# Two token tiles ahead of the adaLN weights, and adaLN weights stored tile by tile

## The chip, the core and the metric

The kernel runs on one core of a Trainium2 chip. Its time is that of one execution on the device in microseconds (us). The median of three runs is 1481.48 us, the lowest 1479.01, the highest 1484.4. The engines are TensorE (PE; its weight loads are listed as PEld), VectorE (DVE), ScalarE (ACT), GpSimd (POOL) and SyncE (SP), which here only issues transfers.

## The reference, cut to what matters

A block of a diffusion transformer over 1024 latent tokens (`x`) and 256 context tokens (`ctx`), 1024 wide, depth 1. All is float32.

```python
sh1, sc1, g1, sh2, sc2, g2 = adaln(c, ada_w, ada_b)          # silu(c) @ ada_w + ada_b, split in six
csh1, csc1, ... = adaln(c_ctx[None, :], ada_w, ada_b)
h_lat = modulate(rms_norm(x, norm_mix_g), sh1, sc1)          # h * (1 + scale) + shift
h_ctx = modulate(rms_norm(x_ctx, norm_mix_g), csh1, csc1)
y = hybrid_mixer(h_ctx, h_lat, w_in, ...)                    # [context ; latent] @ w_in, DeltaNet and retention
x = x + g1 * (y[:, CTX_LEN:] @ w_out)
x = x + g2 * swiglu(modulate(rms_norm(x, norm_ffn_g), sh2, sc2), w_ffn_in, w_ffn_out)
return rms_norm(x, final_g)
```

The change concerns the first lines: the 1024 x 6144 matrix `ada_w` times two conditioning vectors, and the normalised, scaled and shifted tokens that the first projection reads.

## The kernel before, in words

Large products are made from three products of rounded parts: a float32 tile is split into `hi` (rounded to the matmul type by ACT, L344) and `lo` (the difference, by DVE, L345), and PE adds hi\*hi, lo\*hi and hi\*lo (L371 to L373, the tile `tm`). The tokens are handled in ten tiles of 128, of which 0 and 1 are context and 2 to 9 latent, in the groups [2, 3], [4, 5], [6, 7, 8, 9], [0, 1] (`XGROUPS`).

**The order of work.** The program text is laid out by a planner (the TileContext is opened with `schedule_with_timeline_sim=True`): it fixes the order on every engine beforehand by a simulated time, in which text order counts and readiness too, so an engine's queue may differ from the text. Each engine runs its queue in order. Two things are tied by hand. `in_order` (L235) chains the transfers on SP that go through it, so that they are issued in the order of the text; SP transfers that don't go through it (`weights`, L354) are placed among them by the planner. `tc.issue_after` sets one instruction behind another on its engine.

**The first stage.** It needs sixteen adaLN tiles of 128 x 2 x 512 floats (512 KB each). `ada_load(h, k)` (L254) takes, of the rows k\*128 to k\*128+127 of `ada_w`, columns from the shift and from the scale (i) for one half h of the 1024 features. In the matrix a row of the tile is two pieces of 512 floats, 2 KB each. The tiles share six buffers (`adaw`, bufs=6), so from the seventh on a load waits until an earlier tile is used up. `ada_tile(h, k)` (L258) multiplies a tile with the conditioning vectors: for six of the sixteen (`PLAIN`: (0,0), (0,7), (1,0), (1,1), (1,4), (1,7)) by direct float32 products on PE (L266, L268), for the others by an ACT rounding (`adahi`, L273), a DVE difference (`adalo`, L274) and products with both (L277, L278). The last tile of a half completes two PSUM rows; `rows_of` copies them out, `rows_turned` transposes them on PE, and `coefficients` (L293) makes scale and shift of that half on DVE.

`load_x(t)` (L240) loads one token tile of 128 rows of 4 KB, into one of seven buffers. `normalize(0)` squares tiles 2 and 3 on ACT (L325), makes the root (L126, with the loading of an ACT table) and its reciprocal on DVE, and scales the tiles (L328). They are transposed on PE (L334) and copied to `xnT` by DVE and ACT in turn (L422, L424). `modulate` (L307) applies the coefficients for one k and writes `hhi` (ACT, L311) and `hlo` (DVE L313, then DVE or POOL L314).

In the text before, all of half 0 comes first, then the first tile of half 1, then normalising and transposing, the split of the first raw weights, and the modulation of k = 0 to 3, mixed with the rest of half 1. The loads run in the order (0,0) to (0,7), (1,0), x2, x3, (1,1), (1,2), first raw weights, (1,3), (1,4), second raw weights, (1,5) to (1,7). The first product with the projection weights, `begin(2)` (L434, L443), is set behind the last product of tile (1,7); it is the first `tm` product of the kernel. Meanwhile the loads of the second weight group, the tiles 4 and 5 and further tokens follow on SP (L450 to L458). A prefetch of later weights (`wraw<-wg`, L354) shares two `wraw` buffers with the first two raw weights.

**Later adaLN tiles.** `ada_rest` (L488) is called eight times for the other four of the six parts. Each call loads four tiles of 128 x 2 x 512 by SP (L495) and sums them on DVE (L497, L499), beside the projections. There each row of a tile is two pieces of 2 KB too.

Of the kernel before, what the change touches and what calls it, by code (L numbers as in the profile page):

```python
# [17 lines left out]
P = 128  # L18
D = 1024
KT = D // P  # L20
# [18 lines left out]
def build(nc, tc, ap, dbg=None, stop=None, marks=None):  # L39
    root = ExitStack()  # L40
    V, S, G, T, SY = nc.vector, nc.scalar, nc.gpsimd, nc.tensor, nc.sync
# [45 lines left out]
    def bank(tag, name):  # L87
        return PS["pool"].tile([P, 512], F32, tag=tag, name=name, bufs=PS["tags"][tag])
# [4 lines left out]
    def bank_b(name):  # L93
        return bank("pb", name)
# [96 lines left out]
    try:  # L191
# [43 lines left out]
        def in_order(out, src):  # L235

            with tc.issue_after(order[0]) if order[0] is not None else nullcontext():
                order[0] = SY.dma_start(out, src).ins

        def load_x(t):  # L240
            xts[t] = P0.tile([P, D], F32, tag="xt", name="xt", bufs=7)
            in_order(xts[t], ap["ctx"][t * P:(t + 1) * P, :] if t < 2 else ap["x"][(t - 2) * P:(t - 1) * P, :])
# [10 lines left out]

        def ada_load(h, k):  # L254
            w = adaw[h, k] = PA.tile([P, 2, 512], F32, tag="adaw", name="adaw", bufs=6)
            in_order(w, ap["ada_w"][k * P:(k + 1) * P, 0:2 * D].rearrange("p (i e n) -> p i e n", i=2, e=2)[:, :, h, :])

        def ada_tile(h, k):  # L258
            w = adaw[h, k]
            kw = {"skip_group_check": True} if k else {}  # L260
            last = KT - 1
            if (h, k) in PLAIN:

                for i in range(2):
                    if k == 0:
                        T.matmul(psr[h][i][:4, :], cs0, w[:, i], start=True, stop=True)  # L266
                    else:
                        mm = T.matmul(psr[h][i][:2, :], csl[:, k, :], w[:, i], start=False, stop=(k == last), **kw)  # L268
                        done[0] = mm.ins
                return  # L270
            whi = PA.tile([P, 2, 512], F32R, tag="adahi", name="adahi", bufs=3)
            wlo = PA.tile([P, 2, 512], F32R, tag="adalo", name="adalo", bufs=3)
            S.activation(whi, w, AF.Copy)  # L273
            V.tensor_tensor(wlo, w, whi.bitcast(F32), ALU.subtract)  # L274
            for i in range(2):
                o = psr[h][i][:4, :]
                T.matmul(o, cs2[:, k].rearrange("p a b -> p (a b)"), whi[:, i], start=(k == 0), stop=False, **kw)  # L277
                T.matmul(o, cs2[:, k].rearrange("p a b -> p (a b)"), wlo[:, i], start=False, stop=True, **kw)  # L278

        def rows_of(h):  # L280

            rows = [P0.tile([4, 512], F32, tag="hf", name="rows", bufs=2) for _ in range(2)]
            S.activation(rows[0], psr[h][0][:4, :], AF.Copy)
            V.tensor_copy(rows[1], psr[h][1][:4, :])
            return rows

        def rows_turned(h, rows):
            for j in range(8):
                c0 = 32 * h + 4 * j
                last = T.transpose(pst[:, c0:c0 + 4], rows[j // 4][:, j % 4 * P:(j % 4 + 1) * P], ident[:4, :4])  # L290
            return last.ins
# [38 lines left out]
        def turned(gi, k, bank):  # L330

            pt = bank("xtr")
            for i, t in enumerate(XGROUPS[gi]):
                T.transpose(pt[:, i * P:(i + 1) * P], xts[t][:, k * P:(k + 1) * P], ident)  # L334
            return pt[:, :len(XGROUPS[gi]) * P]
# [24 lines left out]
        def tm_weights(g, kh, pl, q=S):  # L360
            return weights(ap["wt"][g, :, 4 * kh:4 * kh + 4, :], [4, 256], V, pl, q, raws.get((g, kh)), g == 0)
# [39 lines left out]
        def fin_copy(t, o, res):  # L401
            S.activation(res, o, AF.Copy)

        for k in range(KT):
            ada_load(0, k)
        for k in range(KT):
            ada_load(1, k)
            if k == 0:
                load_x(2)
                load_x(3)  # L410
            elif k in (2, 4):
                raw_weights(0, k // 4, W)
        for k in range(KT):
            ada_tile(0, k)
        rows = rows_of(0)
        ada_tile(1, 0)
        rows_turned(0, rows)
        normalize(0)
        xnT = P0.tile([P, KT, 256], F32, tag="xnT", name="xnT")
        for k in range(KT):  # L420
            if k % 2:
                V.tensor_copy(xnT[:, k, :], turned(0, k, bank_a))  # L422
            else:
                S.activation(xnT[:, k, :], turned(0, k, bank_a), AF.Copy)  # L424
        wr = {(0, 0): tm_weights(0, 0, W)}
        ada_tile(1, 1)
        coefficients(0)
# [13 lines left out]
        rows = rows_of(1)  # L441
# [43 lines left out]
        ada2 = C.tile([P, 2, KT], F32, tag="ada2", name="ada2")  # L485
        grow = [dr.tile([1, D], F32, tag="grow%d" % i, name="grow%d" % i) for i in range(2)]

        def ada_rest(c, half):  # L488

            c0 = c * D + half * 512  # L490
            acc = R2.tile([P, 512], F32, tag="acc", name="acc", bufs=1)
            for k in range(KT):
                if k % 2 == 0:
                    w = R2.tile([P, 2, 512], F32, tag="adaw2", name="adaw2", bufs=2)
                    SY.dma_start(w, ap["ada_w"][k * P:(k + 2) * P, c0:c0 + 512].rearrange("(a p) n -> p a n", p=P))  # L495
                if k == 0:
                    V.tensor_scalar(acc, w[:, 0], csl[:, k, 0:1], None, ALU.mult)  # L497
                else:
                    V.scalar_tensor_tensor(acc, w[:, k % 2], csl[:, k, 0:1], acc, ALU.mult, ALU.add)  # L499
            ps = bank_b("gr")  # L500
            if c in (2, 5):
                row = R2.tile([1, 512], F32, tag="row", name="row", bufs=1)
                SY.dma_start(row, ap["adarow"][c0:c0 + 512].unsqueeze(0))
                T.matmul(ps[:1, :], ones[:, 0:1], acc, start=True, stop=True)
                V.tensor_tensor(row, row, ps[:1, :], ALU.add)
                SY.dma_start(grow[0 if c == 2 else 1][:, half * 512:(half + 1) * 512], row)
            else:
                for k in range(4):
                    T.matmul(ps[:, 2 * k:2 * k + 2], acc[:, k * P:(k + 1) * P], ones[:, 0:2], start=True, stop=True)
                ks = slice(half * 4, half * 4 + 4)  # L510
                o = ada2[:, c - 3, ks]
                V.tensor_tensor(o, ps[:, 0:8].rearrange("p (k t) -> p k t", t=2)[:, :, 0],
                                adab[:, 8 * c + 4 * half:8 * c + 4 * half + 4], ALU.add)
                if c == 4:
                    V.scalar_tensor_tensor(o, o, 1.0, gffn[:, ks], ALU.add, ALU.mult)
# [938 lines left out]
        w = {}  # L1454
# [156 lines left out]
def prepare(inputs):  # L1611
    f = lambda a: np.ascontiguousarray(np.asarray(a))
    w_in = np.asarray(inputs["w_in"])[0]
    a = {}
    a["x"] = f(inputs["x"])[0]
    a["ctx"] = f(inputs["ctx"])[0]
    a["cc"] = f(np.stack([np.asarray(inputs["c"])[0], np.asarray(inputs["c_ctx"])], -1).reshape(KT, P, 2).transpose(1, 0, 2))
    a["ada_w"] = f(inputs["ada_w"])[0]
    a["adab"] = f(np.asarray(inputs["ada_b"])[0].reshape(48, P).T)
    a["adarow"] = f(inputs["ada_b"])[0]  # L1620
    a["gmix"] = f(np.asarray(inputs["norm_mix_g"])[0].reshape(KT, P).T)
    a["gffn"] = f(np.asarray(inputs["norm_ffn_g"])[0].reshape(KT, P).T)
    col = {"z": 1536, "rq": 2064, "rk": 2576, "rv": 3088, "rg": 3600}
    wt = np.concatenate([w_in[:, col[n]:col[n] + 512] for n in GROUPS], 1)
    a["wt"] = f(wt.reshape(KT, P, 10, 256).transpose(2, 1, 0, 3))
    a["wg"] = f(w_in[:, :1536].reshape(KT, P, 12, P).transpose(2, 1, 0, 3))
    a["wt0"] = f(np.concatenate([wt[:, :256], w_in[:, 2048:2064]], 1).reshape(KT, P, 272).transpose(1, 0, 2))
    a["cw"] = f(np.asarray(inputs["conv_w"])[0].reshape(5, 12, P).transpose(2, 1, 0))
    a["alog"] = f(np.asarray(inputs["gdn_a_log"])[0].reshape(8))
    a["dtb"] = f(np.asarray(inputs["gdn_dt_bias"])[0].reshape(8))  # L1630
    a["gains"] = f(np.stack([np.asarray(inputs["gdn_norm_g"])[0], np.asarray(inputs["ret_norm_g"])[0]], -1))
    a["rdl"] = f(np.asarray(inputs["ret_decay_logit"])[0].reshape(8))
    a["wo"] = f(inputs["w_out"])[0]
    a["wfi"] = f(np.asarray(inputs["w_ffn_in"])[0].reshape(KT, P, 2 * FT, P).transpose(2, 1, 0, 3))
    a["wfo"] = f(inputs["w_ffn_out"])[0]
    a["fg"] = f(inputs["final_g"])
    a.update(_tables())
    return a
# [14 lines left out]
```

## Time and profile before

| what | value |
|---|---|
| median of three runs | 1481.48 us (1479.01 to 1484.4) |
| span of the profiled execution, first to last instruction | 1479.4 us |
| mean granted TensorE clock over the span | 0.983 |
| bytes moved by DMA over the span | 298.14 MB, mean 202 GB/s |
| bytes moved by DMA from 0 to 100 us | 21.34 MB, mean 213 GB/s |
| instructions | 24109 |

How to read it: the share of busy time is a mean over stages that have different limits. Rows of the windows give, for a stretch of time, how long each engine was busy, with the count of instructions in brackets, then the granted TensorE clock (1.00 is full speed), the busy share of the 16 DMA engines and what they moved in GB/s. Rows of the timeline give the start, the duration, the engine, the line, the operation, output<-inputs and shapes; in square brackets is the idle time before it, with what ended it. Rows of groups end in busy time, mean ns of one instruction, and the idle time before them. "SPq" and "ACTq" are the sequencers that issue transfers. A span counts from the first instruction to the last; a run's time is taken on the device for the whole execution, so the two differ a little.

### The profile page before, as it was taken

The page shows a single profiled execution, that of the slowest core. Times are in us where ns is not written, and L with a number is a line of the kernel's source. Part 1 is how long each engine was busy: PE and PEld are TensorE (multiplying, and loading weights), DVE is VectorE, ACT ScalarE, POOL GpSimd, SP SyncE. Part 2 cuts the span into 40 slices and gives each one's busy share as a digit, 9 for nine tenths or more (in the row PEclk, how much of TensorE's full clock was granted, in tenths as well). Part 3 has the DMA queues.
Part 4 walks back from the last instruction along what each step waited for, and adds up shares of the span by engine and source line. Part 5 has one row for each costly group of instructions (what it writes and reads, how often), then busy time and mean ns, then how long its engine had stood idle before and what let it go on. Part 6 is the DMA issues. An engine that isn't in the chain of part 4 may idle for free.

```text
span 1479.4 us, 24109 instructions
## 1 busy us (share of the span) xinstructions
PE 1400.0 (95%) x8919; PEld 1203.0 (81%) x8919; DVE 969.2 (66%) x1856; ACT 613.4 (41%) x1326; POOL 590.5 (40%) x501
## 2 busy tenths in 40 slices
PE   7999999987789999899699899999999999999997
PEld 2898888976789999799588688877888888788886
DVE  6566789289782535579777877646555564657577
ACT  5643564687333111245534533223333332444444
POOL 0120010243201354244144688899555553325321
PEclk9999999999899999999899999999999999999999
DMA  8536686688878723996633265765222242785863
GB/s 323 210 106 203 189 250 199 223 263 279 269 196 271 272 72 118 416 372 204 215 114 115 86 226 208 260 238 178 107 108 107 107 150 76 234 280 193 305 206 114
DMA packets 176565, 298.14 MB, mean 202 GB/s; under 512 B 43496, under 2 KB 93880, under 8 KB 172096
## 3 DMA queue, kind: packets, MB, share of 16 engines
q1 hardware_dynamic: 124896, 253.17, 49.7%
q10 hardware_dynamic: 49072, 35.83, 7.8%
q0 software_dynamic: 2480, 7.60, 1.4%
q8 instruction: 70, 1.15, 0.3%
q14 instruction: 47, 0.39, 0.1%
HBM read 206.60 MB, written 89.96 MB: 200 GB/s over the span
## 4 chain that ended last, share of the span: by engine, by line
PE 55%; POOL 6%; DMA 6%; issue 3%; DVE 2%; ACT 2%; SPq 0%; ACTq 0%; POOLq 0%; DVEq 0%
PE ffn L1344 7%; PE ffn L1342 6%; PE ffn L1343 6%; PE fo L1470 5%; PE fo L1468 5%; PE fo L1469 5%; PE tm L371 3%; PE tm L372 3%; PE tm L373 3%; PE op L1201 2%; PE op L1203 2%; PE op L1202 2%; DMA wd<-tw 1%; POOL ws L1315 1%; PE up L929 1%
## 5 line engine op out<-in xcount | busy, mean ns | idle before, releaser
L371 PE MATMUL tm<-whi,hhi 128*128 128x256 f32 (+1 forms) x704 | 201.5, 290 | 6.1 <-ACT vt L859 2.9
L372 PE MATMUL tm<-wlo,hhi 128*128 128x256 f32 (+1 forms) x704 | 200.8, 287 | 0.3 <-DVE wlo L345 0.3
L373 PE MATMUL tm<-whi,hlo 128*128 128x256 f32 (+1 forms) x704 | 198.6, 286 | 0.0
L371 PEld LDWEIGHTS tm<-whi,hhi 128*128 128x128 f32 x704 | 134.2, 192 | 10.3 <-ACT vt L859 3.1
L344 ACT ACTIVATE whi<-wraw 128x512 fp32r<-128x512 f32 (+2 forms) x98 | 75.2, 771 | 159.7 <-PE ffn L1343 81.9
L1344 PE MATMUL ffn<-t,wlo 128*128 128x512 f32 x352 | 137.1, 390 | 1.4 <-DVE wlo L345 1.4
L1342 PE MATMUL ffn<-t,whi 128*128 128x512 f32 x352 | 137.0, 390 | 1.3 <-ACT whi L344 1.3
L1343 PE MATMUL ffn<-t,whi 128*128 128x512 f32 x352 | 137.0, 389 | 0.0
L372 PEld LDWEIGHTS tm<-wlo,hhi 128*128 128x128 f32 x704 | 135.2, 192 | 2.2 <-issue 0.9
L373 PEld LDWEIGHTS tm<-whi,hlo 128*128 128x128 f32 x704 | 134.3, 192 | 0.7 <-DVE hlo L314 0.2
L344 ACT ACTIVATE whi<-ws 128x512 fp32r<-128x512 f32 x88 | 55.6, 632 | 173.0 <-PE ffn L1343 123.7
L345 DVE TENSOR_TENSOR wlo<-ws,whi 128x512 fp32r<-128x512 f32 x88 | 95.1, 1081 | 45.7 <-ACT whi L344 45.3
L1468 PE MATMUL fo<-whi,ahi 128*128 128x512 f32 x308 | 119.3, 389 | 0.7 <-ACT ahi L344 0.7
L1469 PE MATMUL fo<-wlo,ahi 128*128 128x512 f32 x308 | 119.9, 389 | 0.0
L1470 PE MATMUL fo<-whi,alo 128*128 128x512 f32 x308 | 119.0, 390 | 0.0
L345 DVE TENSOR_TENSOR wlo<-wraw,whi 128x512 fp32r<-128x512 f32 (+2 forms) x92 | 103.4, 1125 | 23.4 <-ACT whi L344 23.2
L1342 PE MATMUL ffn<-b,whi 128*128 128x512 f32 x264 | 103.9, 394 | 4.3 <-ACT whi L344 4.3
L1344 PE MATMUL ffn<-b,wlo 128*128 128x512 f32 x264 | 103.7, 393 | 0.7 <-DVE wlo L345 0.7
L1343 PE MATMUL ffn<-b,whi 128*128 128x512 f32 x264 | 103.7, 393 | 0.0
L612 PE MATMUL b<-hlo,whi 128*128 128x512 f32 (+1 forms) x256 | 94.7, 370 | 0.0
L613 PE MATMUL b<-hhi,wlo 128*128 128x512 f32 (+1 forms) x256 | 94.5, 369 | 0.0
L611 PE MATMUL b<-hhi,whi 128*128 128x512 f32 (+1 forms) x256 | 94.2, 368 | 0.0
(446 smaller groups left out, 3443.7 us busy)
## 6 DMA issues: line engine op xcount, KB each, us to landing
adaw<-ada_w SPq DMA_DIRECT2D x48, 512.0 KB, 4.8
pk<-sd SPq DMA_DIRECT2D x16, 1536.0 KB, 11.6
wraw<-wfi SPq DMA_DIRECT2D x44, 512.0 KB, 3.9
ar<-ad SPq DMA_DIRECT2D x33, 512.0 KB, 4.8
w<-wfo SPq DMA_DIRECT2D x22, 512.0 KB, 5.7
wd<-tw SPq DMA_DIRECT2D x11, 1024.0 KB, 4.8
ad<-act SPq DMA_DIRECT2D x20, 512.0 KB, 3.1
raw<-wd SPq DMA_DIRECT2D x20, 512.0 KB, 4.9
```

The costliest lines, as they stand in the source:

```text
L344: S.activation(hi, raw, AF.Copy)
L345: e.tensor_tensor(lo, raw, hi.bitcast(F32), ALU.subtract)
L371: T.matmul(o, hhi[:, k, tsl], whi[:, k % 4, :], start=(k == 0), stop=False)
L372: T.matmul(o, hhi[:, k, tsl], wlo[:, k % 4, :], start=False, stop=False)
L373: T.matmul(o, hlo[:, k, tsl], whi[:, k % 4, :], start=False, stop=(k == KT - 1))
L612: T.matmul(o, whi[:, k, :], hl, start=False, stop=False)
L1342: T.matmul(o, whi[:, k, :], xhi(xn, slice(0, 4), k), start=(first and k == 0), stop=False, **kw)
L1343: T.matmul(o, whi[:, k, :], xlo(xn, slice(0, 4), k), start=False, stop=False, **kw)
L1344: T.matmul(o, wlo[:, k, :], xhi(xn, slice(0, 4), k), start=False, stop=(k == 3), **kw)
L1468: T.matmul(po[g][i], ahi[:, ts], whi, start=(j == 0 and not kw), stop=False, **kw)
L1469: T.matmul(po[g][i], ahi[:, ts], wlo, start=False, stop=False, **kw)
L1470: T.matmul(po[g][i], alo[:, ts], whi, start=False, stop=(j == FH - 1), **kw)
```

## The change

Three edits:

1. The loads of token tiles 2 and 3 stand ahead of all adaLN loads on SP. The two raw weight loads stand after tiles (1,1) and (1,4), rather than after (1,2) and (1,4).
2. In the text, normalising tiles 2 and 3, their transposes and the copies to `xnT` stand ahead of the adaLN products of half 0.
3. `ada_w` is given to the kernel as two arrays, arranged on the host. `ada1[h, k]` holds the tile (h, k) and `ada2[part, pair]` the tiles of `ada_rest`; each is contiguous, with 4 KB for a partition. The bytes of each load and their number stay the same.

```diff
         def ada_load(h, k):
             w = adaw[h, k] = PA.tile([P, 2, 512], F32, tag="adaw", name="adaw", bufs=6)
-            in_order(w, ap["ada_w"][k * P:(k + 1) * P, 0:2 * D].rearrange("p (i e n) -> p i e n", i=2, e=2)[:, :, h, :])
+            in_order(w, ap["ada1"][h, k])
...
+        load_x(2)
+        load_x(3)
         for k in range(KT):
             ada_load(0, k)
         for k in range(KT):
             ada_load(1, k)
-            if k == 0:
-                load_x(2)
-                load_x(3)
-            elif k in (2, 4):
+            if k in (1, 4):
                 raw_weights(0, k // 4, W)
-        for k in range(KT):
-            ada_tile(0, k)
-        rows = rows_of(0)
-        ada_tile(1, 0)
-        rows_turned(0, rows)
         normalize(0)
         xnT = P0.tile([P, KT, 256], F32, tag="xnT", name="xnT")
         for k in range(KT):
...
                 S.activation(xnT[:, k, :], turned(0, k, bank_a), AF.Copy)
+        for k in range(KT):
+            ada_tile(0, k)
+        rows = rows_of(0)
+        ada_tile(1, 0)
+        rows_turned(0, rows)
         wr = {(0, 0): tm_weights(0, 0, W)}
...
             c0 = c * D + half * 512
+            src = ap["ada2"][2 * (c - 2) + half]
...
-                    SY.dma_start(w, ap["ada_w"][k * P:(k + 2) * P, c0:c0 + 512].rearrange("(a p) n -> p a n", p=P))
+                    SY.dma_start(w, src[k // 2])
...
-    a["ada_w"] = f(inputs["ada_w"])[0]
+    ada_w = np.asarray(inputs["ada_w"])[0]
+    a["ada1"] = f(ada_w[:, :2 * D].reshape(KT, P, 2, 2, 512).transpose(3, 0, 1, 2, 4))
+    a["ada2"] = f(ada_w[:, 2 * D:].reshape(KT // 2, 2, P, 8, 512).transpose(3, 0, 2, 1, 4))
```

## The prediction

> **What bounds the kernel now.** I read the page first. TensorE is busy for nearly the whole span, so only a stretch in which it has no work of the main products can give time back.
>
> ```profile
> span 1479.4 us, 24109 instructions
> PE 1400.0 (95%) x8919; PEld 1203.0 (81%) x8919; DVE 969.2 (66%) x1856; ACT 613.4 (41%) x1326; POOL 590.5 (40%) x501
> ```
>
> Then the windows of 20 us. Of the ten rows from 100 to 300 here are the first and the last: PE is full in all of them (19.97 once), so what comes earlier ahead of 100 moves all of it, and what other engines or the DMA save inside it is worth nothing.
>
> ```profile
> 100.00:120.00 20.00, 20.00 (x140) 18.07 (x139) 17.09 (x29) 7.36 (x13) 2.41 (x1) 1.00 0.78 249
> ...
> 280.00:300.00 20.00, 20.00 (x124) 17.73 (x123) 12.05 (x14) 14.87 (x50) 7.27 (x7) 1.00 0.86 281
> ```
>
> Then the first 55 us in short windows (columns: bounds, length, busy PE, PEld, DVE, ACT, POOL with counts, granted clock, DMA share, GB/s).
>
> ```profile
> 5.00:10.00 5.00, 3.74 (x11) 0.64 (x10) 1.98 (x2) 2.51 (x3) 0.00 (x0) 1.00 1.07 384
> 10.00:15.00 5.00, 3.41 (x13) 0.75 (x12) 4.15 (x4) 3.77 (x4) 0.00 (x0) 1.00 1.04 382
> 15.00:20.00 5.00, 4.71 (x14) 0.95 (x14) 1.90 (x2) 2.04 (x5) 0.00 (x0) 1.00 1.04 399
> 20.00:25.00 5.00, 3.67 (x19) 1.33 (x18) 2.93 (x15) 3.33 (x5) 0.00 (x0) 1.00 1.05 397
> 25.00:30.00 5.00, 3.28 (x19) 1.61 (x17) 5.00 (x10) 4.83 (x10) 1.10 (x1) 1.00 1.03 389
> 30.00:32.50 2.50, 1.73 (x5) 0.34 (x6) 2.50 (x5) 2.50 (x4) 0.72 (x1) 1.00 0.85 244
> 32.50:35.00 2.50, 1.68 (x6) 0.27 (x5) 2.50 (x3) 0.66 (x1) 0.00 (x0) 1.00 0.03 8
> 35.00:37.50 2.50, 2.45 (x8) 0.43 (x7) 0.66 (x1) 0.12 (x1) 0.00 (x0) 1.00 1.05 326
> ...
> 45.00:50.00 5.00, 4.69 (x39) 4.48 (x38) 3.18 (x8) 2.81 (x8) 0.52 (x1) 1.00 1.01 410
> 50.00:52.50 2.50, 2.50 (x24) 2.50 (x23) 0.18 (x1) 0.69 (x2) 0.00 (x0) 1.00 1.04 415
> ```
>
> Two bounds follow each other: until 30 the DMA is full; from 25 to 35 VectorE is full (10.0 of 10.0), while from 32.5 to 35 the DMA carries almost nothing. VectorE was nearly free at 5 to 10 and at 15 to 20. The timeline gives the ends, the tile view of adaw its loads, and the DMA view of 21.5 to 24 the last of them.
>
> ```profile
> 23.33 1.42 DVE L328 TENSOR_SCALAR xt<-xt,rx0y 128x1024 f32<-128x1024 f32 x2
> 31.16 2.00 ACT L273 ACTIVATE adahi<-adaw 128x1024 fp32r<-128x1024 f32 x2
> 32.11 1.28 DVE L345 TENSOR_TENSOR wlo<-wraw,whi 128x1088 fp32r<-128x1088 f32 x1
> 33.31 2.35 DVE L274 TENSOR_TENSOR adalo<-adaw,adahi 128x1024 fp32r<-128x1024 f32 x2
> 35.71 0.63 PE L278 MATMUL ada<-adalo,cs 128*4 128x512 f32 x2
> 36.27 1.88 PE L268 MATMUL ada<-adaw,csl 128*2 128x512 f32 x4
> 38.08 0.39 PE L371 MATMUL tm<-whi,hhi 128*128 128x272 f32 x1
> ```
>
> ```profile
> L238 SPq DMA_DIRECT2D adaw<-ada_w x16: 367/368/480, 0.7 to 23.0; - x16
> ...
> DMA to landing us min/median/max: 4.4/8.3/9.8
> ```
>
> ```profile
> adaw<-ada_w SPq DMA_DIRECT2D x1, 512.0 KB, 8.5
> ```
>
> The last tile, (1,7), is issued at 23.0 and lands 8.5 later, at 31.5. The first main product starts at 38.08. Of these 6.6 us, (1,7) itself needs 1.88 on PE; the rest is VectorE catching up.
>
> **The change part by part.** I name a tile by (half, k), and cost the moved work from the groups of the first 100 us.
>
> ```profile
> L325 ACT ACTIVATE junk<-xt 128x1024 f32<-128x1024 f32 x10 | 10.6, 1057 | 0.2
> L325 ACT ACTIVATION_READ_ACCUMULATOR junk<-xt 128x1 f32 x10 | 1.9, 186 | 0.0
> L126 ACT ACT_TABLE_LOAD x1 | 1.3, 1283 | 0.0
> L126 ACT ACTIVATE rx0s<-ms,epsb 128x2 f32<-128x2 f32 x1 | 0.3, 295 | 0.0
> L422 DVE COPY xnT<-xtr 128x256 f32<-128x256 f32 x4 | 1.7, 417 | 0.0
> L273 ACT ACTIVATE adahi<-adaw 128x1024 fp32r<-128x1024 f32 x10 | 10.4, 1054 | 4.5 <-DMA adaw<-ada_w 4.2 <-PE ada L278 0.3
> L274 DVE TENSOR_TENSOR adalo<-adaw,adahi 128x1024 fp32r<-128x1024 f32 x10 | 12.1, 1220 | 4.5 <-ACT adahi L273 4.3
> ```
>
> *Loads first.* The stage moves the same 20 large loads, so the order alone doesn't move the last landing; x takes the first two places and every early adaLN tile lands two places (about 2.6 us) later. x2 lands at about 0.74 + 4.4 = 5.1, x3 at 6.4, (0,0) at 7.7. SP issues the same number of transfers.
>
> *Rows of 4 KB.* In the rows of 5 to 30, mostly adaLN tiles in rows of 2 KB, the mean is 390 GB/s; at 45 to 52.5, with x and weights in rows of 4 KB, 410 and 415. The 16 tiles are 8.39 MB: 21.5 us at 390, 20.4 at 412. So (1,7) lands at 31.5 - 1.1 = 30.4 (bounds: 31.5 if the rate is not the rows' doing, 29.6 if I count 17 steps of 1.28 and two of 1.36 from 5.1). [...]
>
> *Normalising moved forward.* ACT: two squares with their reads (2.5), a table load (1.28), a root (0.3) and four copies (1.5) leave 18 to 31. DVE: the scaling (1.42), about 0.8 of small root steps and four copies (1.7), some 3.9 us, leave 21 to 32. They run where both waited for the first tiles. On DVE the start is x3 at 6.4, plus 1.24, 1.28 and 0.3 on ACT (the first square fits before x3): 9.3.
>
> *What is late next.* DVE does the same 21.6 us between 5 and 37.5 (the sum of its column). From 9.3 without a pause it would end at 30.9, so it is again close to the bound. Walking it by hand: start work and the six splits of half 0 (7.3) end near 20.5; (0,7) must pass PE before the first coefficients, during which DVE splits (1,2), (1,3) and the first raw weights; coefficients and the first four modulations end near 30; (1,5) ends at 31.2 and (1,6), landed at 29.1 and rounded by 30.2, at 32.4. PE then needs 0.63 + 1.88: first main product at 34.9 rather than 38.08, 3.2 earlier. If the second raw-weight split (1.28) goes ahead of (1,6), it is 36.2, 1.9 earlier. The 4 KB rows are worth about 0.1 of this, since DVE decides.
>
> *The next loads.* The in-order weights of the second group stand on SP behind a prefetch that waits for a raw buffer.
>
> ```profile
> 28.42 5.54 SPq L354 DMA_DIRECT2D wraw<-wg  x2
> 34.06 0.60 SPq L238 DMA_DIRECT2D wraw<-wt  x1
> ...
> 42.73 1.39 POOL L314 TENSOR_TENSOR hlo<-hf,hhi 128x256 fp32r<-128x256 f32 x1 [10.82 <-ACT hhi L311]
> 43.23 0.39 PE L372 MATMUL tm<-wlo,hhi 128*128 128x256 f32 x1 [0.25 <-DVE wlo L345]
> ```
>
> The second raw split (32.11 to 33.39) frees the buffer that the second wg waits for, and that wg holds back wraw at 34.06, which PE needs at 43.23. If DVE does (1,6) first, this load comes no sooner and PE meets the wait later on; if it does the raw split first, the start comes later. So between 1.9 and 3.2 I take 2.5; bounds 0 (the load unmoved, PE in the same order) and 5.0 (below).
>
> *The later adaLN loads* (L487-L499) also become rows of 4 KB. Their 32 transfers end where PE is full, as in the windows above, so I count nothing; without that cover, 32 times 0.07 us (512 KB at 390 against 412), 2.3 us.
>
> ```profile
> L495 SPq DMA_DIRECT2D adaw<-ada_w x32: 367/370/1224, 70.5 to 243.6; - x32
> ```
>
> **Sum:** span 1479.4 - 2.5 = 1476.9. The span is 2.1 under the median shown, 1481.48, and near the lowest of its runs; with that distance kept, 1479.0.
>
> **The rivals.**
>
> *A, DVE keeps up.* DVE is never behind, (1,6) decides: landed at 28.3 (29.6 less a step), 1.05 + 1.22 + 0.63 + 1.88 later PE starts, at 33.1, 5.0 earlier: 1476.5. For it: DVE's sum allows 30.9. Against: DVE must wait for coefficients in the middle. [...]
>
> *B, given back.* The start moves, but the weights of the second group land as before and PE waits for them: 1481.5. For it, the SP order above; against it, whi of the second raw half will be ready earlier, as ACT is emptier at 25 to 30.
>
> *C, transposes ahead of adaLN on PE: slower.* The new text puts the transposes of x before the first adaLN product. If PE's queue keeps that order, PE idles from 5.3 to about 11.5 and (0,0) runs at 14.0 to 15.9. All six adaLN buffers are full at 14.1; the next load goes out at 15.9 and lands 4.4 later at 20.3, not 15.4: the stream is 4.9 late, (1,7) lands at 35.3, and by the same steps PE starts at about 38.8, 0.8 late. A clock loss comes on top.
>
> ```profile
> 375.86 2.40 PE L856 MATMUL vT<-ident,y 128*128 128x128 f32 x10 [8.52 <-ACT y L624]
> ```
>
> ```profile
> 378.00:380.00 2.00, 2.00 (x12) 2.00 (x11) 1.79 (x7) 0.86 (x4) 0.38 (x1) 0.50 1.07 315
> ```
>
> After 8.52 us without work PE ran at a granted clock of 0.50. Five such microseconds lose 2.5, part of it under the DMA stall; I take 1.2 of it and 2.0 in all: 1483.5 (bounds +0.8 and +3.3). [...] What decides is whether the first transpose of x stands before the first adaLN product on PE. Against C: before, ACT rounded adaLN tiles ahead of copies that the text has earlier, so the planner orders by readiness.
>
> *D, another order far behind.* The planner lays out the whole program by simulated time, so another first stage can change orders later. The wait of 8.52 in front of vT above shows what one bad place costs there: the same again would give 1479.0 + 8.5 = 1487.5, and as much can be won, 1470.5.
>
> **How the numbers follow.** Forecast 0.45, A 0.22, B 0.13, C 0.10, D 0.10, both signs alike. Its own range is 1476.5 to 1481.5. About 0.3%, 4.4 us, is what a measurement of this kernel can tell from no change. Faster by more than that, below 1477.0: two thirds of A (0.15), a sixth of the forecast (0.07) and half of D (0.05), 0.27. Slower, above 1485.9: half of D (0.05), a third of C with its clock loss in full and late transfers on top (0.03), and 0.03 for a run of medians as wide apart as those shown, 0.11. The rest, 0.62, is within. The range takes in the forecast, A, B and C: 1474.5 (A with the landing's other half microsecond and the spread of the runs) to 1484.5.
>
> **What would show it.** In the changed kernel: the squares of x near 5 to 8, not 18; adaLN landings of 1.28 us apart and GB/s above 405 in the windows of 10 to 30, else the rows do nothing; the last DVE split ending near 32.4 and the first tm product near 34.9 (33.1 for A, 38 or later for C, with PE empty from 5.3 to 11); wraw of the second group issued near 34 and a PE wait of over 1 us on wlo or whi before 50 for B; PE full from about 90 to 297, and the distance to the end of the span unchanged from there, else D. The forecast is wrong if SP puts the wg prefetch before the last adaLN loads, as then (1,7) lands 1.3 later, or if DVE's order leaves it idle in the middle of the stage.

## The result, and the profile after

The changed kernel takes 1479.47 us in the median of 20 runs (1475.23 to 1482.47); the kernel before, run beside it, takes 1483.35 (1479.01 to 1486.09). The ratio is 0.9973 with a 95% interval of 0.9964 to 0.9983: a gain of 4.0 us. The forecast was 1479.0 from 1481.48, a gain of 0.17%, and 0.27% was measured: near in the number, but the profile shows that the gain isn't where the forecast put it. All ratios compare fast runs with fast runs; one execution each of e1, e9, e10 and e11 took 1747 us or more, counts as slow and is left out of them.

The head of the page of after, to set beside the two lines of before: the span is 3.2 us shorter, and every engine has the same count of instructions as before.

```profile
span 1476.2 us, 24111 instructions
PE 1397.2 (95%) x8919; PEld 1199.2 (81%) x8919; DVE 964.6 (65%) x1856; ACT 614.0 (42%) x1326; POOL 590.3 (40%) x501
```

The first stage of after in the windows that the prediction used (busy PE, PEld, DVE, ACT, POOL with counts, granted clock, DMA share, GB/s):

```profile
5.00:10.00 5.00, 2.84 (x5) 0.37 (x4) 0.68 (x4) 3.55 (x6) 0.00 (x0) 1.00 1.02 384
10.00:15.00 5.00, 4.65 (x13) 0.84 (x12) 3.78 (x7) 4.70 (x6) 0.00 (x0) 1.00 1.03 410
15.00:20.00 5.00, 4.64 (x25) 2.23 (x26) 4.98 (x7) 2.48 (x5) 0.00 (x0) 1.00 0.97 359
20.00:25.00 5.00, 5.00 (x16) 1.14 (x15) 2.65 (x5) 2.55 (x4) 0.00 (x0) 1.00 0.98 388
25.00:30.00 5.00, 4.55 (x21) 1.34 (x20) 3.92 (x12) 2.96 (x4) 0.00 (x0) 1.00 0.98 348
30.00:32.50 2.50, 1.62 (x4) 0.17 (x2) 2.46 (x5) 2.50 (x5) 1.64 (x1) 1.00 0.75 278
32.50:35.00 2.50, 0.71 (x3) 0.17 (x4) 2.50 (x5) 1.05 (x2) 0.77 (x1) 1.00 0.82 259
35.00:37.50 2.50, 2.45 (x9) 0.47 (x9) 1.00 (x1) 0.00 (x0) 0.00 (x0) 1.00 0.93 300
```

The normalising did move: VectorE has 4.98 of 5 at 15 to 20, where before it had 1.90. But from 30 to 35 it is as full as before, and the DMA, which was to be the first bound until 30, falls to 359 and 348 GB/s in two of the rows. The timeline of after shows the end of the stage:

```profile
23.41 1.29 DVE L345 TENSOR_TENSOR wlo<-wraw,whi 128x1088 fp32r<-128x1088 f32 x1 [2.24 <-ACT whi L344]
27.76 0.24 DVE L298 TENSOR_TENSOR adaT<-adaT,adab 128x8 f32<-128x8 f32 x2 [1.02 <-PE adaT L290]
29.59 2.08 ACT L311 ACTIVATE hhi<-xnT,bmix,amix 128x256 fp32r<-128x256 f32 x4 [1.06 <-DVE bmix L304]
30.19 1.29 DVE L345 TENSOR_TENSOR wlo<-wraw,whi 128x1088 fp32r<-128x1088 f32 x1
31.57 1.99 ACT L273 ACTIVATE adahi<-adaw 128x1024 fp32r<-128x1024 f32 x2
33.12 2.88 DVE L274 TENSOR_TENSOR adalo<-adaw,adahi 128x1024 fp32r<-128x1024 f32 x2
36.61 1.88 PE L268 MATMUL ada<-adaw,csl 128*2 128x512 f32 x4
38.42 0.40 PE L371 MATMUL tm<-whi,hhi 128*128 128x272 f32 x1
```

The last two adalo pieces end at 36.0 (35.7 before), and the first main product starts at 38.42: 0.34 later than before, not 3.2 earlier. VectorE spent the time that the normalising had freed in the two bracketed waits (2.24 for the first raw weights, 1.02 for the coefficients), and ScalarE split tiles (1,5) and (1,6) only behind four hhi tiles, which wait for the same coefficients. These came late through TensorE: in the timeline of after it has no idle time from 17.76 to 28.7 us, and the products that complete half 0, those of (0,7), are the first four of the eight in the second line here, behind 2.9 us of the hoisted transposes and behind tile (1,0) (first line).

```profile
20.52 1.88 PE L266 MATMUL ada<-adaw,cs 128*4 128x512 f32 x4
22.89 3.60 PE L268 MATMUL ada<-adaw,csl 128*2 128x512 f32 x8
```

So where do 4 us come from? The line view gives the first and last start of a group. L611 is the last convolution product, L834 the last of the merges, L1081 stands at the end of the scan over the chunks. First before, then after:

```profile
L611 PE MATMUL b<-hhi,whi x256: 276/392/481, 111.1 to 351.2; 128*128 128x512 f32 x96, 128*128 128x256 f32 x32
L834 PE MATMUL m<-U,xt x160: 218/218/267, 430.4 to 477.4; 64*64 64x64 f32 x160
L1081 PE MATMUL ro<-Rf,qk x64: 275/275/421, 646.7 to 716.4; 128*128 128x128 f32 x64
```

```profile
L611 PE MATMUL b<-hhi,whi x256: 276/392/481, 111.4 to 350.7; 128*128 128x512 f32 x96, 128*128 128x256 f32 x32
L834 PE MATMUL m<-U,xt x160: 218/218/267, 426.0 to 473.3; 64*64 64x64 f32 x160
L1081 PE MATMUL ro<-Rf,qk x64: 274/275/421, 641.8 to 710.9; 128*128 128x128 f32 x64
```

The first L611 starts 0.3 later, as the first tm product did. From 351.2 to 716.4 before takes 365.2 us, after takes 360.2 from 350.7 to 710.9: five microseconds are won there, where no line of the diff has any work. (Behind 716.4 and 710.9, these two profiles differ by 2.3 us the other way.) Set side by side, the two programs have the same order on every engine from about 40 to 380 us, and another one from there to about 680: 1037 of the 7698 places on TensorE hold another instruction. The planner made that order; nobody wrote it. That is the mechanism of rival D.

### The profile page after: what moved, and what is told of

The parts are those of the page before. It is cut to its first block, busy times and chain, and to the rows that moved or that the text cites. A ratio compares the mean times of both kernels' runs of the same rounds, so it can differ in the third digit from the quotient of the medians.

```text
span 1476.2 us, 24111 instructions
## 1 busy us (share of the span) xinstructions
PE 1397.2 (95%) x8919; PEld 1199.2 (81%) x8919; DVE 964.6 (65%) x1856; ACT 614.0 (42%) x1326; POOL 590.3 (40%) x501
## 4 chain that ended last, share of the span: by engine, by line
PE 55%; POOL 6%; DMA 5%; DVE 4%; issue 2%; ACT 2%; SPq 1%; ACTq 0%; POOLq 0%; DVEq 0%
PE ffn L1344 7%; PE ffn L1342 6%; PE ffn L1343 6%; PE fo L1470 4%; PE fo L1469 4%; PE fo L1468 4%; PE tm L371 3%; PE tm L373 3%; PE tm L372 3%; PE op L1203 2%; PE op L1201 2%; PE op L1202 2%; DMA wd<-tw 2%; POOL ws L1315 1%; DMA pk<-sd 1%
## 5 line engine op out<-in xcount | busy, mean ns | idle before, releaser
L371 PE MATMUL tm<-whi,hhi 128*128 128x256 f32 (+1 forms) x704 | 199.5, 287 | 7.7 <-ACT vt L859 3.4
L372 PE MATMUL tm<-wlo,hhi 128*128 128x256 f32 (+1 forms) x704 | 199.3, 285 | 2.4 <-issue 2.0
L371 PEld LDWEIGHTS tm<-whi,hhi 128*128 128x128 f32 x704 | 132.8, 190 | 11.8 <-ACT vt L859 3.6
L372 PEld LDWEIGHTS tm<-wlo,hhi 128*128 128x128 f32 x704 | 133.7, 190 | 2.1 <-issue 0.9
L345 DVE TENSOR_TENSOR wlo<-wraw,whi 128x512 fp32r<-128x512 f32 (+2 forms) x92 | 99.4, 1082 | 24.6 <-ACT whi L344 24.6
L611 PE MATMUL b<-hhi,whi 128*128 128x512 f32 (+1 forms) x256 | 94.3, 368 | 0.0
```

The lines of the kernel that those rows point to most:

```text
L345: e.tensor_tensor(lo, raw, hi.bitcast(F32), ALU.subtract)
L371: T.matmul(o, hhi[:, k, tsl], whi[:, k % 4, :], start=(k == 0), stop=False)
L372: T.matmul(o, hhi[:, k, tsl], wlo[:, k % 4, :], start=False, stop=False)
```

## The experiments

Theory 1: the other order from 380 us on makes the gain. Rivals: the rows of 4 KB (theory 2), or the hoisted loads and normalising (theory 3). Set side by side, rows alone leave every engine's order as it was, and the hoist alone produces the whole later order of after. So rows and hoist were tried alone, and the order by itself was then put on the kernel before and taken off the kernel after.

**e1, rows alone.** The kernel before with

```
-  in_order(w, ap["ada_w"][k * P:(k + 1) * P, 0:2 * D].rearrange(...)[:, :, h, :])
+  in_order(w, ap["ada1"][h, k])
...
-  SY.dma_start(w, ap["ada_w"][k * P:(k + 2) * P, c0:c0 + 512].rearrange("(a p) n -> p a n", p=P))
+  SY.dma_start(w, src[k // 2])
```

> The kernel before with nothing but the two adaLN weight arrays laid out tile by tile in rows of 4 KB. Every engine keeps the order of before to the end. Theory 1 (the gain of the whole change, -4.0 us, sits in the different order of work between 360 and 680 us): no gain, ratio 1.000 within 0.001, and the last L834 product within 1 us of before. Theory 2 (the gain is that of the 4 KB rows): ratio 0.997. Theory 3 (the gain is that of loading and normalising x first): ratio 1.000.

Measured: 0.9996 (0.9980 to 1.0012), no gain. The rate did rise, as the windows of e1 show against 382, 399 and 397 GB/s before:

```profile
10.00:15.00 5.00, 4.15 (x16) 0.90 (x14) 4.27 (x4) 2.97 (x3) 0.00 (x0) 1.00 1.04 413
15.00:20.00 5.00, 4.69 (x19) 1.28 (x20) 0.94 (x2) 3.02 (x6) 0.00 (x0) 1.00 1.02 409
20.00:25.00 5.00, 3.66 (x16) 1.28 (x16) 4.00 (x16) 3.17 (x5) 0.00 (x0) 1.00 1.03 412
```

The first tm product starts at 37.0 here; in the profiles of before and of the three kernels that keep its first stage and its rows (e4, e5, e6) it starts at 37.8 to 38.3. One profile shows about 1 us won in the first stage; the total doesn't resolve it. The last L834 product was expected within 1 us of before, and it came 2.3 us earlier (475.1 against 477.4): single profiles differ by this much with the same order.

**e2, the hoist alone.** The kernel after with the two old lines of `ada_w` in place of `ada1` and `ada2`.

> The kernel after, with the adaLN weights in their old rows of 2 KB: only the loads of x and the normalising are ahead. Every engine has the order of after to the end. Theory 1 (later order): ratio 0.997, with the last L834 product about 4 us ahead of before. Theory 2 (rows): ratio 1.000. Theory 3 (front): ratio 0.997, and then the first product of the first stage's tokens ought to start earlier than 38.08 us.

Measured: 0.9961 (0.9946 to 0.9977). The gain is there, but the first tm product starts at 38.9, 0.8 later than before; with rows of 4 KB it is 38.4 in after against 37.0 in e1. So the hoist made the first stage about 1 us longer in these profiles. Theory 2 has fallen; theory 3 fails its own condition. Theory 1 has the ratio, but not its other sign: the last L834 product should have come 4 us earlier and came at 477.9, 0.5 later than before. What e2 calls the hoist takes in the move of the first raw weight load by one tile (edit 1 of the change).

**e3 and e4, the order alone.** Edges without a wait tie each instruction of the stretch to its predecessor in a written list (cut here; the lists run to 38 lines in e4 and 94 in e3), so that the planner must issue in that order:

```
+    ORDER = ["""5109 5094+11 5110+19 ...
+    for chain in ORDER:
+        prev = None
+        for run in chain.split():
+            first, more = (int(v) for v in (run + "+0").split("+")[:2])
+            for n in range(first, first + more + 1):
+                if prev is not None:
+                    tc.add_manual_dep(by["I-%d" % n], prev, nosync, reason="order")
+                prev = "I-%d" % n
```

e3 is after with the later order of before, e4 is before with the later order of after.

> The kernel after, whole, with the instructions from about 380 us on put back by hand into the order that they had before; the first stage stays that of after. Theory 1 (later order): the gain is gone, ratio 1.000 (first product 0.3 us late). Theory 2 (rows) and theory 3 (front): the gain stays, ratio 0.997.

> The kernel before, whole, with the instructions from about 380 us on put by hand into the order that they have in after; first stage and rows of 2 KB stay those of before. Theory 1 (later order): ratio 0.997 or a little lower, the last L834 product 4 us earlier, the products of 365 to 430 us with less idle time ahead of them. Theory 2 (rows) and theory 3 (front): ratio 1.000.

Measured: e3 0.9992 (0.9974 to 1.0011), e4 0.9974 (0.9956 to 0.9992). In e4 the last L834 product came 2.2 us earlier, not 4. In the profile of e3 the first tm product starts at 40.0, 1.6 later than in after, so a part of its missing gain may be that; but e2, which has the hoist too and the new order, took 1479.0 us in the median on the same chip, and e3 1484.4. The gain goes with the order both ways: off when the whole change stays and only the order goes back, on when nothing of the change is there but the order. Theory 1 is shown by the times; the position of L834 in single profiles doesn't bear it out as forecast.

**e5 and e6, which half.** The kernel before with the new order to about 478 us only (inversion and merges), and from there only (scan over the chunks).

> The kernel before, with the new order only from about 380 to 478 us (the inversion and merging of the blocks), and the old order put back by hand from 478 us on. Theory 1a (the gain is the shorter wait of PE ahead of m<-U,xt at L814 while DVE works on the inversion): most of the gain is here, ratio 0.998, idle time ahead of L814 4 us or less instead of 5 to 6. Theory 1b (the gain is the shorter waits ahead of up<-vn,pk and kS<-S,pk after 478 us): ratio 1.000. Each half has some 2 us of the 4.4 us by which the stretch from 351 to 716 us is shorter in the three traces with the new order, so I expect about half of the gain in each.

> The kernel before, with its own order to 478 us and the new order only from there to about 680 us (the scan over the chunks). Theory 1a: ratio 1.000. Theory 1b: ratio 0.998, idle time ahead of L929 1.5 us instead of 3. About half of the gain is expected here.

Measured: e5 0.9982 (0.9968 to 0.9996), e6 0.9980 (0.9964 to 0.9996). Half of the gain is in each, as expected. The profiles agree in the second half: from the last L834 to the last L1081 start, the kernels with the old order there (before, e1, e3, e5) take 237.6 to 239.3 us, those with the new one (after, e2, e4, e6, e7, e8) 234.2 to 237.6. The groups of that stretch say what got shorter. Before:

```profile
L922 PE MATMUL Tr<-r,pk 128*128 128x128 f32 x144 | 21.1, 284 | 2.2 <-DVE r L917 2.2
L929 PE MATMUL up<-vn,pk 128*128 128x128 f32 x144 | 19.3, 279 | 3.2 <-ACT vn L924 3.2
L914 PE MATMUL kS<-S,pk 128*128 128x128 f32 x144 | 18.6, 275 | 1.7 <-DMA pk<-sd 1.7
L814 PE MATMUL m<-U,xt 32*32 32x32 f32 x320 | 5.3, 205 | 6.1 <-issue 6.1
```

and e6 (the last number before the arrow is the idle time ahead of the group, and behind it stands who ended it):

```profile
L922 PE MATMUL Tr<-r,pk 128*128 128x128 f32 x144 | 21.8, 283 | 2.9 <-DVE r L917 2.9
L929 PE MATMUL up<-vn,pk 128*128 128x128 f32 x144 | 18.9, 277 | 1.8 <-ACT vn L924 1.8
L914 PE MATMUL kS<-S,pk 128*128 128x128 f32 x144 | 18.5, 276 | 0.1
```

1.4 us are won ahead of `up`, 1.6 ahead of `kS` (the new order issues two loads of pk on SP ahead of smaller ones), and 0.7 lost ahead of `Tr`: 2.3 of the 4.8 us by which e6 is shorter than before here (239.0 to 234.2). In the first half my mechanism, theory 1a, falls. The wait ahead of L814 does shrink in e5, but it comes back ahead of another product:

```profile
L372 PE MATMUL tm<-wlo,hhi 128*128 128x256 f32 x416 | 119.1, 288 | 5.2 <-issue 5.2
L814 PE MATMUL m<-U,xt 32*32 32x32 f32 x320 | 5.3, 202 | 2.0 <-issue 2.0
```

7.2 us for both, against 6.1 before. That this half gives something is measured (0.9982, interval below 1); through which wait isn't settled, and e5's own profile, at 126.2 us from the last L611 to the last L834 start, is no shorter than before.

**e7 and e8, why the first stage gave nothing.** F1: a load of convolution weights (wg) slipped ahead of the last adaLN load on SP. F2: TensorE stood still, then ran slowly, and gave its buffers back late. e7 holds that load:

```
+        last_ada = order[0]
...
+                with tc.issue_after(hold) if hold is not None else nullcontext():
+                    q.dma_start(raw[:, :, :n], src)
```

and e8 has `range(3)` for `range(2)` in the warm-up products. Both keep the later order of after.

> The kernel after, with the first load of convolution weights held on SP until the last adaLN weight load is issued; every other engine keeps the order of after. Theory F1 (the front gave nothing because this load of 512 KB went ahead of the last adaLN tile): the last tile lands about 1.3 us earlier, at 31.8, and the first product of the tokens starts at about 37.1 instead of 38.4. Theory F2 (it gave nothing because TensorE idled 2.2 us ahead of its first adaLN product, ran at half speed after that and so gave the six weight buffers back late): the last load is issued no earlier than its buffer is free, the first product stays within 0.5 us of 38.4. Total time within 0.2% of after either way.

> The kernel after, with a third warm-up product on the zero tile, so that TensorE is busy from 5.3 to about 7.2 us; every engine keeps its order otherwise. Theory F2: the first adaLN products take 600 ns instead of 1046, TensorE is 2 us further at 15 us, the weight buffers come free earlier, and the first product of the tokens starts at 36 to 37. Theory F1: the products are faster but the first product of the tokens stays within 0.5 us of 38.4. Total time 0 to 2 us below after.

Measured: e7 0.9970 (0.9955 to 0.9985), first tm product at 38.6; its last adaLN load is issued at 26.7 against 26.5 in after, because it waits for its buffer and not for wg (see the landing of (1,7) below). F1 has fallen. e8 0.9974 (0.9958 to 0.9989). Its adaLN products of tile (0,0) take 590 ns instead of 1046, as F2 has it, but VectorE's last adalo starts at 33.16, against 33.12 in after: what TensorE lost at the beginning was hidden. The first tm product came at 40.0, since TensorE ran slowly in front of it (0.66 granted clock in the row of 35 to 40, and this line of the timeline, 1.88 in after):

```profile
37.04 3.01 PE L268 MATMUL ada<-adaw,csl 128*2 128x512 f32 x4
```

So F2 has fallen too. What is left is VectorE itself (F3).

**e9, VectorE's order in the first stage.** The kernel after, with both wg loads behind the x loads, and a written order (with the code of e3 and e4) for nine instructions of ScalarE and sixteen of VectorE, here by their tiles:

```
-  ACT   whi(0,1) | hhi x4 | adahi(1,5) | adahi(1,6)
+  ACT   whi(0,1) | adahi(1,5) | hhi x2 | adahi(1,6) | hhi x2
-  DVE   hf x2 | wlo(0,1) | hlo | hf x2 | hlo | adalo(1,5) | adalo(1,6)
+  DVE   hf | adalo(1,5) | hlo | hf | adalo(1,6) | hf x2 | hlo | wlo(0,1)
```

> The kernel after with three changes in the first stage and its own order kept from 380 us on: ScalarE splits adaLN tile (1,5) ahead of the four hhi tiles and (1,6) after two of them; VectorE does adalo of these two ahead of the third to fifth modulating steps and of the second wlo of the token weights; both early loads of convolution weights go behind the x loads on SP. Theory F3 (the first stage is set by VectorE, which is full from 25.5 to 36.0 us with adalo of (1,6) as its last piece, behind 1.3 us of wlo and 1.4 us of modulating that the first product doesn't need): the first product of the tokens starts at 35.5 instead of 38.4 us, and the total is 2 to 3 us below after, ratio 0.995 to before. Theory F4 (something else holds the first product, as the landing of the last tile or the granted clock): it stays above 37.5 us and the total is that of after, 0.997.

Measured: 0.9945 (0.9928 to 0.9962), from five executions. The timeline of e9 (its L372 is the L371 of after):

```profile
29.94 1.22 DVE L274 TENSOR_TENSOR adalo<-adaw,adahi 128x1024 fp32r<-128x1024 f32 x1
31.81 1.22 DVE L274 TENSOR_TENSOR adalo<-adaw,adahi 128x1024 fp32r<-128x1024 f32 x1
34.35 1.81 DVE L345 TENSOR_TENSOR wlo<-wraw,whi 128x1088 fp32r<-128x1088 f32 x1
33.64 1.88 PE L268 MATMUL ada<-adaw,csl 128*2 128x512 f32 x4
35.45 0.39 PE L372 MATMUL tm<-whi,hhi 128*128 128x272 f32 x1
```

The first main product starts at 35.45, where 35.5 was expected, and everything up to 365 us lies 2.3 to 2.9 us ahead of before. F3 holds: with this order VectorE is done earlier, and the first product comes as forecast. The edit also reorders ScalarE, whose pieces VectorE waits for, and moves both wg loads; the three weren't tried apart (e7 held one of the wg loads alone and won nothing).

**e10, a number that should do nothing.** The kernel before, with one digit changed in the loads of the first stage:

```
-            elif k in (2, 4):
+            elif k in (1, 4):
                 raw_weights(0, k // 4, W)
```

> The kernel before with one number changed: the first raw token weights are loaded one adaLN tile earlier. In the first stage eight positions on TensorE and seven on VectorE differ, but from 400 us on 1504 of 7698 positions on TensorE do: a third later order. Theory 1 (the later order makes the difference, and any small edit of the first stage draws a new one): the time differs from before by some us in either direction, ratio between 0.995 and 1.005, with the first product of the tokens within 0.5 us of 38.1. If instead the later orders of small edits all cost the same, ratio 1.000 within 0.001, and the gain of the change would be something special to its order.

Measured: 0.9965 (0.9952 to 0.9977), as large as the whole change. Its first tm product starts at 37.9 and its last L611 at 351.6, against 38.1 and 351.2 before, so nothing is won up to there. In its profile 2.0 us are won from 351 to 716 us, and 4.0 lost again behind that, so I have no place for the measured gain beyond "after 351 us" (the profiled execution, 1483.57 us, is the slowest of the eleven). This digit is itself a piece of the change, so after has it too, with yet another order. Which piece of the edit draws which order wasn't looked for.

**e11 and e12, is the hoist needed?** e11 undoes the hoist (rows of 4 KB kept), holds the two wg loads as e9 does, and writes the order of ScalarE and VectorE by the same idea; from 380 us on it has the order of after. e12 is e9 again.

> The loads and the normalising of x put back to their places of before (rows of 4 KB kept), and the first stage reordered by the idea of e9: adalo of (1,5) and (1,6) on VectorE, and adahi of both on ScalarE, ahead of what the first product doesn't need, both early loads of convolution weights behind the x loads; from 380 us on the order of after. Theory F5 (with the order right, the hoist of x is worth nothing: VectorE has the pieces up to adalo of (1,6) done at about 33 us by the durations of before): first product at 35.4, total that of e9, ratio 0.995. Theory F6 (the hoist becomes worth its 3.9 us of VectorE once the order lets it): first product at 37 or later, total 1.5 to 3 us above e9.

> The kernel of e9 once more, on the same chip as e11, for the comparison of these two: first product at 35.5, ratio 0.995 to before. Theory F5: the same time as e11 within 1 us. Theory F6: 1.5 to 3 us below it.

Measured: e11 0.9948 (0.9926 to 0.9969), e12 0.9959 (0.9943 to 0.9975). First main product at 35.30 and 35.60:

```profile
35.30 0.40 PE L372 MATMUL tm<-whi,hhi 128*128 128x272 f32 x1
```

F5 holds: with the right order the loads of before do as well. The reordered kernels are faster than before in all three runs. Against after (0.9973, 0.9964 to 0.9983) only the interval of e9 lies clear, those of e11 and e12 overlap it, and no run sets them side by side.

All kernels, ratios to the kernel before:

| | first stage | order from 380 us | first tm product, us | ratio |
|---|---|---|---|---|
| before | old | old | 38.1 | 1 |
| after | hoist, 4 KB | new | 38.4 | 0.9973 |
| e1 | 4 KB | old | 37.0 | 0.9996 |
| e2 | hoist | new | 38.9 | 0.9961 |
| e3 | hoist, 4 KB | old | 40.0 | 0.9992 |
| e4 | old | new | 38.3 | 0.9974 |
| e5 | old | new to 478 | 37.9 | 0.9982 |
| e6 | old | new from 478 | 37.8 | 0.9980 |
| e7 | hoist, 4 KB, wg later | new | 38.6 | 0.9970 |
| e8 | hoist, 4 KB, warm-up | new | 40.0 | 0.9974 |
| e9, e12 | hoist, 4 KB, reordered | new | 35.5, 35.6 | 0.9945, 0.9959 |
| e10 | one tile earlier | a third | 37.9 | 0.9965 |
| e11 | 4 KB, reordered | new | 35.3 | 0.9948 |

(e3 and e8 have a granted clock of 0.66 in the row of 35 to 40 us, e4 one of 0.66 in that of 30 to 35; what brought it was not shown.)

## Why the prediction was right in its number and wrong in its place

That 1479.0 lies so near 1479.47 is luck. The 2.5 us of the sum were to come from the first stage, which gave nothing, and the base of 1481.48 was 1.9 below the median of before that the result is compared with.

- *Where time can be won.* "What comes earlier ahead of 100 moves all of it": right. e9 brought its first product 2.6 us forward, and at 351 us it was still 2.3 ahead.
- *Loads first, normalising moved.* The squares ran at 6.40 and 7.58 ("5 to 8"). That the work would move ahead was right (its last copy ends at 21.2, where it reached to 31.4 before); that this would shorten the stage was not.
- *Rows of 4 KB.* Forecast 412 GB/s against 390, measured 409 to 413 in e1, against 382 to 399 in the same three windows of before. So the rows do what was said. "About 0.1 of this" was too little where the rows stand alone: e1's first product came about 1 us earlier, although the time shows nothing of it.
- *The landing of (1,7) at 30.4.* It failed: the stream didn't stay full. In after the load was issued at 26.52, 3.5 later than before, and landed 6.6 later, at 33.1. I named the wg prefetch as the danger; it did go first, and e7 shows that it wasn't the reason. A load also needs one of six buffers, and the waits on SP's queue in after name the products that free them (L266 for 3.4 us, L268 for 2.6). The last one decides: the eight L268 products of (0,7) and (1,1) end at 26.49, and the load goes out at 26.52. e8 made the first products faster, but these eight end at 26.52 there, and the load goes out at 26.55. So the queue of TensorE in the middle of the stage holds the load, and not its slow start.
- *The first main product at 34.9.* This is the step that failed, and it was the whole sum of 2.5 us: it was 38.42. The walk let VectorE go on without a pause: the splits of half 0 "end near 20.5", which they did, and coefficients and four modulations "near 30". But the coefficients were ready at 29.6 only, by the order of work on TensorE, and meanwhile VectorE stood still for 2.24 us (first raw weights) and 1.02 (transposed rows). On top, the planner put the second wlo (1.29) ahead of both last tiles, the late piece that the walk had priced at 1.3 (36.2). Without that piece the start would have been about 37.1 (38.42 - 1.29, an estimate from the rows of after). So of the 3.5 us that were missed some 2.2 come from the pauses that the walk left out, and 1.3 from the piece that it named. The prediction's last line had the sign for it, "if DVE's order leaves it idle in the middle of the stage". e9 has the same two waits (2.17 and 1.02) and still starts at 35.45, because it does (1,5) and (1,6) ahead of a part of the modulating that the walk had in front of them: near the forecast start, by another order than the one walked.
- *A and B* didn't occur, as the start never moved. *C* needs TensorE empty to 11; it stood from 5.30 to 7.45. But slow products, whose loss I had counted in C's sum only, came without C (those of (0,0) took 1046 ns in after, 590 in e8); in after they cost nothing at the end of the stage (last adalo at 33.12, and at 33.16 in e8 without them). A milder form of C did occur: the transposes and (1,0) stood ahead of (0,7) on TensorE, and the coefficients came late.
- *D, another order far behind,* is what happened: 0.10, with both signs, for a mechanism that gave all of the gain. Its size, 8.5 by one wait ahead of vT (L856), was twice too large, and its place was wrong: that wait stayed (8.7 before, 9.3 after, between 351 and 716 us), and the gain is on both sides of 478 us. The text had the test for it, whether the distance from the full stretch to the end stays unchanged. It is the line that I should have weighed most, since nothing bounded the sign.

## What to carry to other kernels

Where a planner orders the program, compare the order of the two programs before the times: an edit of the first stage can move work hundreds of microseconds later, and here that was worth 0.3%, as much as one changed digit gave (e10). To learn what an edit itself is worth, hold the rest of the order fixed, and to learn what the order is worth, put it alone on the old kernel. And when work of a bound engine is moved ahead, look at what it then waits for and which piece it does last: here moving 3.9 us ahead gave nothing, and doing two tiles ahead of what wasn't needed yet brought the first product forward by nearly 3 us, with the moved work or without it.

## What the runs showed of the hardware

TensorE stood still for 2.1 to 2.5 us ahead of its first adaLN product in the six traces with the hoist and two warm-up products (after, e2, e3, e7, e9, e12), and a slow stretch followed in each. In e3 and e2 the windows show it: the granted clock was 0.68 and 0.64 in the rows of 7.5 to 10 and 10 to 12.5 us of e3, and 0.55 in the row of 12.5 to 15 us of e2. In after it is in the durations, while the windows show a granted clock of 1.00 (first line: 5 to 20 us of after; second: the same of e8, where the pause is 1.2):

```profile
L266 PE MATMUL ada<-adaw,cs 128*4 128x512 f32 x4 | 3.6, 1046 | 2.2 <-DMA adaw<-ada 2.2
```

```profile
L266 PE MATMUL ada<-adaw,cs 128*4 128x512 f32 x4 | 1.9, 590 | 1.2 <-DMA adaw<-ada 1.2
```

So it is in e7, e9 and e12, with 1045, 1012 and 1046 ns for the same four products and windows of 1.00. In after the 1.00 says nothing of these products: the clock records that are kept with its trace begin at 13.21 us, behind them. Until then its products ran as slowly as the warm-up ones (1061 ns each): two of L278 took 1.05 us from 11.77 on, and two took 0.63 from 13.56 on. So in this trace a window that says 1.00 doesn't prove full speed; the mean duration of a known product shows more.

The sum of the forecast has no term for this. The pauses and the slow stretches behind them are measured in these six traces; whether the pause alone brings a slow stretch, and from what length on, was not shown.
